# Hybrid decoder block on one core: the gate projections of two branches with three of eight pairs of k-tiles by Strassen's scheme

## The chip, the core and the metric

The kernel runs on one core of one Trainium2 chip, as a single launch. The metric is the device time of one execution in microseconds; lower is better. Before the change three runs gave 1595.34 us in the median (1595.19 to 1596.83).

## What is computed

One layer of a hybrid decoder block on x, 256 tokens of 2048 channels, with 256 memory tokens. All arrays are f32. Cut to what matters here:

```
h = rms_norm(x, g_mix_pre)
a_val, a_gate, sb, sc, sx, q, gates = split(h @ w_in)        # gates: three times 2048 columns

a = causal_depthwise_conv(a_val * sigmoid(a_gate), conv_a_w) + conv_a_b     # 31 taps
a = silu(layer_norm(a))
y_a = a @ w_a_out                                            # branch 0
y_b = (sb * causal_depthwise_conv(sc * sx, conv_b_w)) @ w_b_out   # branch 1, 3 taps
y_x = attention(q, memory) @ w_x_out                         # branch 2

g = sigmoid(gates)
merged = g[0] * y_a + g[1] * y_b + g[2] * y_x
x = x + rms_norm(merged @ w_o, g_mix_post)
x = x + rms_norm(relu(rms_norm(x) @ w_up)**2 @ w_down, g_mlp_post)
```

The three gate projections are [256, 2048] @ [2048, 2048] each, the three output products of the branches [256, 1024] @ [1024, 2048].

## The kernel before, in words

**Three products for one.** Every f32 operand of a matmul is split in an upper and a lower part that TensorE takes as fp32r: the upper one is a cast on ScalarE, the lower one the difference on VectorE. For weights `fetch_next` (L93) does this: SP loads a unit (two k-tiles of 128 rows by 512 columns) into a tile `raw`, ScalarE casts it to `wh` (L100), VectorE subtracts to `wl` (L101). For activations `split` (L221 to L223) does it. A product of a k-tile is then three matmuls: upper by upper, upper by lower, lower by upper.

**What sets the order.** The units are planned in the order in which they are used (`plan` L83, and the plan section behind L228). `in_unit` (L134) asks for a unit and fetches LOOK = 4 units ahead of it, in an order raised by PRIO; the tile framework then fixes each engine's instruction list when the kernel is built, and an engine runs its own list strictly in order. `raw` has RAW = 4 buffers, `wh` and `wl` five each. Between units, `between` (L119) issues one of the callables in `steps` and up to three taps of the long convolution (`tap` L449, the multiply-add L455), which are VectorE work on 128 x 256. `drain` (L130) issues all that is left in `steps`.

**The stages.** Queries, the conformer's inputs, keys, values and attention come first. Then branch 2 (L531) runs, then the short convolution (loop behind L531): per half i it projects `sc`, `sx` and `sb` into four banks each (`channels_first`), VectorE computes the three taps (L552 among them), adds the two halves of each `sb` bank (`halves`, L216 to L219), multiplies and splits into `uT[i]`. Then branch 1 (L607) and branch 0 (L627), the output projection and the MLP.

**A branch** (L522). `gates(b, n)` multiplies the 256 tokens by 512 gate columns over 16 k-tiles into two banks (`tokens_first`) and ScalarE takes the sigmoid (L507). `out_of(b, n)` multiplies the branch's activations by 512 columns over 8 k-tiles into two banks, and VectorE multiplies by the gate (L517 or L519) and adds (L520). The order is lagged: the gates of n + 1 stand ahead of the output product of n, so that in branch 0 the order is gates 0, gates 1, out 0, gates 2, out 1, and so on.

**LayerNorm of branch 0.** Behind branch 1 the remaining taps are issued, and then eight steps (L610) are appended: sum over channels (L573), mean by a matmul against ones and its subtraction (L579, L580), squares, variance, scale, sigmoid and gain (L600, L601), and the split into `aT[0]` and `aT[1]` (L223). They are issued between the units of the first gate blocks of branch 0, and `drain` issues the rest ahead of out 0.

```
    def branch(b, act, behind=lambda n: None):
        s = gates(b, 0)
        for n in range(4):
            s, last = gates(b, n + 1) if n < 3 else None, s
            if n == 0:
                drain()
            out_of(b, n, act, last)
            behind(n)
```

Of the kernel before, what the change touches and what calls it, by code (L numbers as in the profile page):

```python
# [15 lines left out]
P = 128  # L16
D = 2048
# [22 lines left out]
TAPS = 3  # L40
LOOK = 4
PRIO = 400
RAW = 4
# [3 lines left out]
def tile_hybrid_block(ctx, tc, x, head, xT, mem, memT, vecs, w_in, w_a_out, w_b_out, w_kv, w_x_out, w_o,  # L47
# [5 lines left out]
    big = ctx.enter_context(tc.tile_pool(name="big", bufs=14))  # L53
# [29 lines left out]
    def plan(w, row0, col0, nk=KD, sizes=None, gain=None):  # L83
        """[nk*128, 512] of w as units of some k-tiles each."""
# [53 lines left out]
    def mm_channels(acc, k, nk, wh, wl, a, ts=None):  # L138
        """Adds k-tile k to four banks, [128 columns of w, 256 tokens] in two halves each."""
# [75 lines left out]

    def halves(b, dst):  # L216
# [602 lines left out]
```

## Time and profile before

| what | value |
|---|---|
| median of three runs | 1595.34 us |
| the profiled execution, its span | 1595.4 us |
| TensorE busy | 1578.8 us, 7950 instructions |
| VectorE busy | 1096.3 us, 1621 instructions |
| ScalarE busy | 781.4 us, 1100 instructions |
| granted TensorE clock, mean | 0.998 |

The span is the time from the first to the last instruction of the profiled execution; no other time is given for that execution. PE is TensorE, DVE VectorE, ACT ScalarE, POOL GpSimd, SP SyncE, which issues the loads. In a timeline each row is a start, a length, the engine, the line of the kernel, the operation, output<-input tiles, their shapes and how many equal instructions the row joins; in brackets stands how long the engine had been idle before it, and what released it. A row that joins n instructions has the length from the first one's start to the last one's end.

### The profile page before, as it was taken

To read this page: it belongs to the slowest core of one execution; us is meant where nothing else is said; L and a number is where in the kernel's file an instruction comes from. 1 tells how busy PE (TensorE), PEld (TensorE's weight loads), DVE (VectorE), ACT (ScalarE), POOL (GpSimd) and SP (SyncE) were. 2 spreads that over 40 slices of the span, in tenths; PEclk is the share of its full clock that TensorE was granted. 3 is DMA by queue.
4 is the path that set the end of the run, shared out by engine and by line. 5 is a ranking of instruction groups with operands and counts; after the bars stand their busy time and mean duration, and the time that the engine had idled before them with its cause. 6 is when DMAs were issued, how large, how long until landed. Compare 5 with 4: busy or idle time off the path is not lost.

```text
span 1595.4 us, 21000 instructions
## 1 busy us (share of the span) xinstructions
PE 1578.8 (99%) x7950; PEld 1338.8 (84%) x7950; DVE 1096.3 (69%) x1621; ACT 781.4 (49%) x1100; POOL 7.6 (0%) x19
## 2 busy tenths in 40 slices
PE   8999999999999999999999999999999999999997
PEld 6888888888888888888888888888888888888886
DVE  6988787777898775775656775457755676567755
ACT  7654455443444444454445654455534554355542
POOL 0000000000000000000000000000000000000000
PEclk9999999999999999999999999999999999999999
DMA  8765655566666666666755665666666666666563
GB/s 274 218 212 185 192 165 172 174 196 189 189 188 187 189 194 197 185 187 191 263 191 168 204 190 190 194 190 185 188 194 197 185 185 192 192 191 188 188 193 111
DMA packets 158694, 305.64 MB, mean 192 GB/s; under 512 B 9473, under 2 KB 13825, under 8 KB 158081
## 3 DMA queue, kind: packets, MB, share of 16 engines
q1 hardware_dynamic: 158592, 304.30, 62.2%
q8 instruction: 62, 1.02, 0.3%
q14 instruction: 40, 0.32, 0.1%
HBM read 302.17 MB, written 2.10 MB: 191 GB/s over the span
## 4 chain that ended last, share of the span: by engine, by line
PE 98%; DVE 1%; DMA 0%; issue 0%; SPq 0%; ACT 0%; POOL 0%; POOLq 0%; DVEq 0%; ACTq 0%
PE bank L76 97%; DMA raw<-in_w_in 0%; DVE t L660 0%; PE bank L622 0%; DVE t L733 0%; DVE wl L106 0%; PE bank L668 0%; DVE t L223 0%; PE bank L420 0%; POOL y L320 0%; DVE t L647 0%; DVE wl L101 0%; ACT wh L100 0%; POOLq L815 0%; SPq L96 0%
## 5 line engine op out<-in xcount | busy, mean ns | idle before, releaser
L76 PE MATMUL bank<-wh,t 128*128 128x512 f32 (+1 forms) x2592 | 794.9, 387 | 0.0
L101 DVE TENSOR_TENSOR wl<-raw,wh 128x1024 fp32r<-128x1024 f32 (+1 forms) x433 | 528.1, 1221 | 366.4 <-ACT wh L100 364.5
L100 ACT CAST wh<-raw 128x1024 fp32r<-128x1024 f32 (+1 forms) x433 | 454.6, 1051 | 575.6 <-PE bank L76 513.7
L76 PE MATMUL bank<-t,wh 128*128 128x512 f32 (+1 forms) x1936 | 681.6, 398 | 4.7 <-ACT wh L100 4.7
L76 PEld LDWEIGHTS bank<-wh,t 128*128 128x128 f32 x2592 | 484.5, 188 | 97.9
L76 PE MATMUL bank<-t,wl 128*128 128x256 f32 (+1 forms) x1936 | 538.9, 281 | 1.6 <-ACT t L291 1.0
L76 PE MATMUL bank<-wl,t 128*128 128x512 f32 (+1 forms) x1296 | 500.9, 387 | 0.0
L76 PEld LDWEIGHTS bank<-t,wh 128*128 128x128 f32 x1936 | 364.1, 189 | 90.3 <-ACT wh L100 4.7
L76 PEld LDWEIGHTS bank<-t,wl 128*128 128x128 f32 x1936 | 367.4, 190 | 5.6 <-DVE wl L101 1.6
L76 PEld LDWEIGHTS bank<-wl,t 128*128 128x128 f32 x1296 | 243.4, 188 | 49.0
L106 DVE SCALAR_TENSOR_TENSOR wl<-raw,vec,wh 128x512 fp32r<-128x512 f32 x256 | 180.9, 748 | 88.8 <-ACT wh L105 86.7
L105 ACT ACTIVATE wh<-raw,vec 128x512 fp32r<-128x512 f32 x256 | 171.6, 717 | 138.5 <-PE bank L76 102.1
L455 DVE SCALAR_TENSOR_TENSOR t<-a_pad,vec,t 128x256 f32<-128x256 f32 x240 | 103.4, 478 | 0.0
L218 ACT COPY s<-bank 128x256 f32<-128x256 f32 x128 | 46.0, 366 | 15.8 <-PE bank L76 15.5
L219 DVE TENSOR_TENSOR s<-bank,s 128x256 f32<-128x256 f32 x128 | 52.3, 417 | 0.0
L222 ACT CAST t<-s 128x256 fp32r<-128x256 f32 x96 | 37.6, 400 | 23.3 <-DVE s L750 15.3
L223 DVE TENSOR_TENSOR t<-s,t 128x256 fp32r<-128x256 f32 x96 | 39.5, 419 | 6.4 <-ACT t L222 5.7
L748 DVE SCALAR_TENSOR_TENSOR s<-s,rm_bc 128x256 f32<-128x256 f32 x64 | 27.2, 426 | 2.2
L750 DVE TENSOR_TENSOR s<-s 128x256 f32<-128x256 f32 x64 | 27.1, 424 | 1.8
L507 ACT ACTIVATE s<-bank,y 128x512 f32<-128x512 f32 x24 | 16.4, 685 | 10.6 <-PE bank L76 10.6
L725 DVE TENSOR_TENSOR t<-bank,t 128x512 f32<-128x512 f32 (+1 forms) x25 | 15.7, 663 | 6.3 <-PE bank L76 6.3
L291 ACT ACTIVATE t<-t,vec 128x256 fp32r<-128x256 f32 x31 | 13.6, 498 | 4.2 <-DMA t<-in_memT 2.6
(105 smaller groups left out, 303.3 us busy)
## 6 DMA issues: line engine op xcount, KB each, us to landing
raw<-in_w_in SPq DMA_DIRECT2D x191, 512.0 KB, 3.8
raw<-in_w_up SPq DMA_DIRECT2D x128, 512.0 KB, 3.7
raw<-in_w_down SPq DMA_DIRECT2D x128, 512.0 KB, 3.7
raw<-in_w_kv SPq DMA_DIRECT2D x32, 512.0 KB, 3.8
raw<-in_w_o SPq DMA_DIRECT2D x32, 512.0 KB, 3.7
raw<-in_w_x_out SPq DMA_DIRECT2D x16, 512.0 KB, 3.9
raw<-in_w_b_out SPq DMA_DIRECT2D x16, 512.0 KB, 4.8
raw<-in_w_a_out SPq DMA_DIRECT2D x16, 512.0 KB, 4.0
```

What stands on the lines that cost most here:

```text
L76: nc.tensor.matmul(o, a, b, start=start, stop=stop)
L100: nc.scalar.copy(h, raw)
L101: pace[0] = nc.vector.tensor_tensor(l, raw, h.bitcast(F32), ALU.subtract).ins
L105: nc.scalar.mul(h[:, j, :], raw[:, j, :], g)
L106: pace[0] = nc.vector.scalar_tensor_tensor(l[:, j, :], raw[:, j, :], g, h[:, j, :].bitcast(F32), ALU.mult, ALU.subtract).ins
L218: nc.scalar.copy(t, b[:, T:])
L219: nc.vector.tensor_tensor(dst, b[:, :T], t, ALU.add)
L222: nc.scalar.copy(dst_h, src)
L223: nc.vector.tensor_tensor(dst_l, src, dst_h.bitcast(F32), ALU.subtract)
L455: nc.vector.scalar_tensor_tensor(conv[:, c, :], src, w, conv[:, c, :], ALU.mult, ALU.add)
L748: nc.vector.scalar_tensor_tensor(s, s, 0.0, r2_bc, ALU.max, ALU.mult)
L750: nc.vector.tensor_tensor(q, s, s, ALU.mult)
```

## The change

Branch order and block size change for all three branches; Strassen's scheme is used in branches 1 and 0.

- **Blocks of 1024 columns.** `gates(b, n)` and `out_of(b, n)` now take 1024 columns each, n = 0 and 1, with four accumulators (two token halves by two column halves), and they alternate: gates 0, out 0, gates 1, out 1. The lag is gone. The weights come in rows, one k-tile of 1024 columns for two k-tiles of 512, with the same size and number of loads. `RAW` is 5 in place of 4. The pool `big` has 13 buffers in place of 14: the gate s is a tile of `big` now, and a late constant `gq` uses the space of `a_pad`.
- **Three triples of k-tiles.** In a gate block of branches 1 and 0, k-tiles j and j + 8 for j = 0, 1, 2 are multiplied as 2 x 2 blocks with seven products in place of eight (the form of Strassen's scheme with common sums). With a the tokens (two halves t) and W the weights (two column halves q), the seven products are a(j, t0) W(j, q1) in `P1`; a(j+8, t0) W(j+8, q1) added to `C11`; form 3 by W(j+8, q0) added to `C12`; and form 0, 2, 1 and a(j+8, t1) by the four weight sums in `Q5`, `P7`, `P6` and added to `C21`. So a block has eight accumulators, all eight PSUM banks.
- **Weight sums.** `fetch_row` makes the four sums of 512 columns of a triple on VectorE (L125, L126, L129, L130), in two tiles that are then cast and split as any unit (L136, L137). Of the row "first" only one column half is used and split.
- **Forms of the tokens.** `x_forms`, once, ahead of branch 1: two additions that join upper and lower part of six k-tiles (L615), four sums and differences (L617 to L620), and a split (L329, L330) into `fh` and `fl`. It is appended to `steps` and drained before the first gate block.
- **Gathering.** `gather` (L306 to L320) adds the eight accumulators to the four results: two copies on ScalarE and eight additions or differences of 512 columns on VectorE; behind each of the four results stands its sigmoid on ScalarE.

```
+SUMMED = 3
+ORDER = (("row", 3), ("row", 11), ("first", 0), ("row", 4), ("second", 0), ("row", 5), ("sums_a", 0), ("row", 6),
+         ("sums_b", 0), ("first", 1), ("row", 7), ("second", 1), ("row", 12), ("sums_a", 1), ("row", 13), ("sums_b", 1),
+         ("first", 2), ("row", 14), ("second", 2), ("row", 15), ("sums_a", 2), ("sums_b", 2))
+TQ = ((0, 1), (0, 0), (1, 1), (1, 0))
-RAW = 4
+RAW = 5
...
-    big = ctx.enter_context(tc.tile_pool(name="big", bufs=14))
+    big = ctx.enter_context(tc.tile_pool(name="big", bufs=13))
...
+    def fetch_row(w, r0, c0, what):
...
+        if what[:4] == "sums":
+            a, b = held["first"], held["second"]
+            if what == "sums_a":
+                nc.vector.tensor_tensor(raw[:, 0], a[:, 0], a[:, 1], ALU.add)
+                nc.vector.tensor_tensor(raw[:, 1], a[:, 0], b[:, 0], ALU.add)
+                held["sums"] = raw
+            else:
+                nc.vector.tensor_tensor(raw[:, 0], held["sums"][:, 0], b[:, 0], ALU.add)
+                nc.vector.tensor_tensor(raw[:, 1], raw[:, 0], b[:, 1], ALU.add)
+        else:
+            nc.sync.dma_start(raw, w[r0:r0 + P, c0:c0 + 2 * NC5].rearrange("p (c n) -> p c n", c=2))
+            held[what] = raw
+            if what == "first":
+                part = slice(1, 2)
+        nc.scalar.copy(h[:, part], raw[:, part])
+        pace[0] = nc.vector.tensor_tensor(l[:, part], raw[:, part], h[:, part].bitcast(F32), ALU.subtract).ins
+        ready.append([(h[:, q], l[:, q]) for q in range(2)])
...
+    def block(rows, act, half, forms=None):
...
+        for n, (what, k, u) in enumerate(rows):
+            if what == "row":
+                todo += [(u, n, f"C{t + 1}{2 - q}", tile_of(k, t), q) for t, q in TQ]
+            elif what == "first":
+                todo.append((u, n, "P1", tile_of(k, 0), 1))
+            elif what == "second":
+                todo += [(u, n, "C11", tile_of(k + half, 0), 1), (u, n, "C12", form(k, 3), 0)]
+            elif what == "sums_a":
+                todo += [(u, n, "Q5", form(k, 0), 0), (u, n, "P7", form(k, 2), 1)]
+            else:
+                todo += [(u, n, "P6", form(k, 1), 0), (u, n, "C21", tile_of(k + half, 1), 1)]
...
+    def gather(acc, dst, put):
+        p1, u3 = (sm.tile([P, NC5], F32, tag="u512", name=name("u"), bufs=4) for _ in range(2))
+        nc.scalar.copy(dst(1, 0), acc["C22"])
+        nc.scalar.copy(p1, acc["P1"])
+        nc.vector.tensor_tensor(dst(0, 1), acc["C11"], p1, ALU.add)
+        put(0, 1)
+        nc.vector.tensor_tensor(p1, acc["P6"], p1, ALU.add)
+        nc.vector.tensor_tensor(u3, acc["P7"], p1, ALU.add)
+        nc.vector.tensor_tensor(dst(1, 1), acc["C21"], u3, ALU.add)
+        put(1, 1)
+        nc.vector.tensor_tensor(p1, acc["Q5"], p1, ALU.subtract)
+        nc.vector.tensor_tensor(dst(0, 0), acc["C12"], p1, ALU.add)
+        put(0, 0)
+        nc.vector.tensor_tensor(u3, acc["Q5"], u3, ALU.subtract)
+        nc.vector.tensor_tensor(dst(1, 0), dst(1, 0), u3, ALU.add)
+        put(1, 0)
...
+            g_gate[b, n] = plan_rows(w_in, C_G + b * D + n * 2 * NC5, ORDER if b < 2 else rows_of(16), 8)
+            g_y[b, n] = plan_rows(w, n * 2 * NC5, rows_of(8), 4)
...
+    def x_forms():
+        both, f = t8([P, 2, SUMMED, T]), t8([P, SUMMED, 4, P])
+        for i in range(2):
+            hl = xt[2 * i]
+            nc.vector.tensor_tensor(both[:, i], hl[:, :SUMMED, 0, :].bitcast(F32), hl[:, :SUMMED, 1, :].bitcast(F32), ALU.add)
+        a11, a21, a12, a22 = (both[:, i, :, t * P:(t + 1) * P] for i in range(2) for t in range(2))
+        nc.vector.tensor_tensor(f[:, :, 0, :], a21, a22, ALU.subtract)
+        nc.vector.tensor_tensor(f[:, :, 1, :], f[:, :, 0, :], a11, ALU.subtract)
+        nc.vector.tensor_tensor(f[:, :, 2, :], a11, a21, ALU.subtract)
+        nc.vector.tensor_tensor(f[:, :, 3, :], a12, f[:, :, 1, :], ALU.add)
+        fh, fl = t8([P, SUMMED, 4, P], F32R), t8([P, SUMMED, 4, P], F32R)
+        split(f, fh, fl)
+        xf.extend([fh, fl])
...
+        for n in range(2):
+            s = gates(b, n)
             if n == 0:
                 drain()
-            out_of(b, n, act, last)
-            behind(n)
+            out_of(b, n, act, s)
+            behind(2 * n)
+            behind(2 * n + 1)
...
+    steps.append(x_forms)
+    drain()
     branch(1, pair(uT))
```

**Excerpt one: VectorE's list where the short convolution ends and branch 1 begins.** Before: `bank_818` to `bank_821` are the four accumulators of the last `sb` projection, L219 adds their halves, L561 multiplies, L223 makes the lower part of `uT`, L101 that of a weight unit, L455 is a tap.

```order
L219 TENSOR_TENSOR s_847_4807<-bank_818_4614,s_848_4808 128x256
L561 TENSOR_TENSOR s_847_4807<-s_847_4807,t8_817_4597 128x256
L101 TENSOR_TENSOR wl_862_4858<-raw_860_4855,wh_861_4857 128x1024
L223 TENSOR_TENSOR t8_846_4806<-s_847_4807,t8_846_4806 128x256
L219 TENSOR_TENSOR s_849_4814<-bank_819_4615,s_850_4815 128x256
L219 TENSOR_TENSOR s_851_4821<-bank_820_4616,s_852_4822 128x256
L561 TENSOR_TENSOR s_849_4814<-s_849_4814,t8_817_4597 128x256
L561 TENSOR_TENSOR s_851_4821<-s_851_4821,t8_817_4597 128x256
L101 TENSOR_TENSOR wl_865_4879<-raw_863_4876,wh_864_4878 128x1024
```

The change, from the two sums of a weight row (L125, L126) on: L330 with `t8_844` is the lower part of `uT`, `t8_853` and `t8_854` are `both` and `f` of x_forms, `t8_855` and `t8_856` are `fh` and `fl`, L559 is a tap.

```order
L326 TENSOR_TENSOR s_849_4819<-bank_818_4614,s_850_4820 128x256
L326 TENSOR_TENSOR s_851_4826<-bank_819_4615,s_852_4827 128x256
L692 TENSOR_TENSOR s_849_4819<-s_849_4819,t8_815_4595 128x256
L692 TENSOR_TENSOR s_851_4826<-s_851_4826,t8_815_4595 128x256
L615 TENSOR_TENSOR t8_853_4833<-t8_2_77 128x768
...
L619 TENSOR_TENSOR t8_854_4834<-t8_853_4833 128x3x128
L617 TENSOR_TENSOR t8_854_4834<-t8_853_4833 128x3x128
...
L618 TENSOR_TENSOR t8_854_4834<-t8_854_4834,t8_853_4833 128x3x128
...
L620 TENSOR_TENSOR t8_854_4834<-t8_853_4833,t8_854_4834 128x3x128
...
L330 TENSOR_TENSOR t8_856_4842<-t8_854_4834,t8_855_4841 128x1536
```

The instructions of x_forms stand behind the last `sb` banks, and the lower part of the forms ends this piece; from the first of the four `sb` banks to it there are 28 instructions.

**Excerpt two: TensorE's list in the first gate block of branch 1.** `t8_2` and `t8_22` are k-tiles 0 to 3 and 8 to 11 of the tokens, `bank_861` to `bank_892` accumulators. Before, where the block begins:

```order
L76 MATMUL bank_821_4617<-t8_30_155,wh_832_4689 128x512
L76 MATMUL bank_855_4835<-wh_835_4714,t8_2_77 128x512
L76 MATMUL bank_855_4835<-wl_836_4715,t8_2_77 128x512
L76 MATMUL bank_855_4835<-wh_835_4714,t8_2_77 128x512
L76 MATMUL bank_856_4836<-wh_835_4714,t8_2_77 128x512
```

The change, 63 matmuls behind the block's first one:

```order
L83 MATMUL bank_866_4872<-wh_876_4919,t8_22_132 128x512
L83 MATMUL bank_866_4872<-wl_877_4920,t8_22_132 128x512
L83 MATMUL bank_866_4872<-wh_876_4919,t8_22_132 128x512
L83 MATMUL bank_865_4865<-wh_859_4847,t8_855_4841 128x512
L83 MATMUL bank_865_4865<-wl_860_4848,t8_855_4841 128x512
L83 MATMUL bank_884_4958<-wh_869_4890,t8_855_4841 128x512
L83 MATMUL bank_884_4958<-wl_870_4891,t8_855_4841 128x512
L83 MATMUL bank_865_4865<-wh_859_4847,t8_856_4842 128x512
```

The block took only the tokens' own tiles before; now its 22nd product reads the upper part of the forms (`t8_855`), and four matmuls later one reads the lower part (`t8_856`), the last result in excerpt one.

**Excerpt three: VectorE's list where the LayerNorm of branch 0 ends.** Before: L600 is the gain, L601 the last pass over all channels, L223 makes the lower part of `aT[0]` and `aT[1]`, L519 and L520 are the gated sum of out_of(0, 0).

```order
L600 TENSOR_SCALAR t8_37_190<-t8_37_190,vec_70 128x256 x4
L601 TENSOR_TENSOR t8_37_190<-t8_37_190,t8_1072_6026 128x2048
L101 TENSOR_TENSOR wl_1078_6065<-raw_1076_6062,wh_1077_6064 128x1024
L101 TENSOR_TENSOR wl_1082_6086<-raw_1080_6083,wh_1081_6085 128x1024
L223 TENSOR_TENSOR t8_1079_6080<-t8_37_190,t8_1079_6080 128x4x256
L101 TENSOR_TENSOR wl_1085_6104<-raw_1083_6101,wh_1084_6103 128x1024
L223 TENSOR_TENSOR t8_1086_6119<-t8_37_190,t8_1086_6119 128x4x256
```

The change; L434 is the copy of the scale over all partitions, L724 its pass, L731 and L732 are L600 and L601, L310 to L313 additions of `gather`, and L330 with `t8_1149` is the lower part of `aT[0]`.

```order
L434 COPY s_1126_6116<-bank_1127_6117 128x256
L724 TENSOR_TENSOR t8_37_190<-t8_37_190,s_1126_6116 128x2048
L137 TENSOR_TENSOR wl_1148_6217<-raw_1146_6215,wh_1147_6216 128x1024
L137 TENSOR_TENSOR wl_1152_6238<-raw_1150_6236,wh_1151_6237 128x1024
L137 TENSOR_TENSOR wl_1155_6250<-raw_1153_6248,wh_1154_6249 128x1024
L731 TENSOR_SCALAR t8_37_190<-t8_37_190,vec_70 128x256
L137 TENSOR_TENSOR wl_1161_6281<-raw_1159_6279,wh_1160_6280 128x1024
L731 TENSOR_SCALAR t8_37_190<-t8_37_190,vec_70 128x256 x7
L732 TENSOR_TENSOR t8_37_190<-t8_37_190,t8_1142_6176 128x2048
L310 TENSOR_TENSOR t8_1067_5881<-bank_1071_5888,u_1156_6260 128x512
L312 TENSOR_TENSOR u_1156_6260<-bank_1107_6031,u_1156_6260 128x512
L330 TENSOR_TENSOR t8_1149_6230<-t8_37_190,t8_1149_6230 128x4x256
```

Before, two gate blocks of 512 columns stood ahead of the first product with `aT`; now one block of 1024 columns does, and two additions of its gathering have come in front of the lower part of `aT[0]`.

## Rows read from the trace of the kernel before

**Rows 1.** The page: busy time by engine, and shares of the chain that ended last.
```profile
PE 1578.8 (99%) x7950; PEld 1338.8 (84%) x7950; DVE 1096.3 (69%) x1621; ACT 781.4 (49%) x1100; POOL 7.6 (0%) x19
...
PE 98%; DVE 1%; DMA 0%; issue 0%; SPq 0%; ACT 0%; POOL 0%; POOLq 0%; DVEq 0%; ACTq 0%
```

**Rows 2.** TensorE's timeline in a gate block of branch 0, first and last row.
```profile
743.06 0.62 PE L76 MATMUL bank<-wh,t 128*128 128x512 f32 x2
...
773.67 0.61 PE L76 MATMUL bank<-wh,t 128*128 128x512 f32 x2
```

**Rows 3.** VectorE's timeline: one row of each kind of instruction.
```profile
501.49 0.61 DVE L552 TENSOR_SCALAR t<-t,vec 128x256 f32<-128x256 f32 x2
...
521.18 0.75 DVE L219 TENSOR_TENSOR s<-bank,s 128x256 f32<-128x256 f32 x2
...
537.20 1.27 DVE L455 SCALAR_TENSOR_TENSOR t<-a_pad,vec,t 128x256 f32<-128x256 f32 x3
...
576.75 3.86 DVE L573 TENSOR_REDUCE s<-t 128x256 f32<-128x2048 f32 x1
580.53 3.48 DVE L101 TENSOR_TENSOR wl<-raw,wh 128x1024 fp32r<-128x1024 f32 x3
...
645.96 1.28 DVE L519 TENSOR_TENSOR s<-bank,s 128x512 f32<-128x512 f32 x2
...
684.34 2.29 DVE L601 TENSOR_TENSOR t<-t,t 128x2048 f32<-128x2048 f32 x1
686.55 2.35 DVE L101 TENSOR_TENSOR wl<-raw,wh 128x1024 fp32r<-128x1024 f32 x2
```

**Rows 4.** Timelines of VectorE and TensorE where branch 1 begins.
```profile
491.53 1.22 DVE L101 TENSOR_TENSOR wl<-raw,wh 128x1024 fp32r<-128x1024 f32 x1 [1.60 <-ACT wh L100]
...
518.91 0.42 DVE L219 TENSOR_TENSOR s<-bank,s 128x256 f32<-128x256 f32 x1
...
515.69 0.39 PE L76 MATMUL bank<-wh,t 128*128 128x512 f32 x1
```

**Rows 5.** Windows: length; busy PE, PEld, DVE, ACT, POOL; PEclk; DMA share; GB/s.
```profile
658.00:691.00 33.00, 33.00 (x151) 27.41 (x150) 29.37 (x30) 20.78 (x26) 0.69 (x1) 1.00 0.57 178
```

**Rows 6.** Timelines of VectorE and ScalarE around the LayerNorm of branch 0.
```profile
657.76 0.42 DVE L579 TENSOR_SCALAR s<-bank 128x256 f32<-128x256 f32 x1 [0.84 <-PE bank L76]
...
690.70 0.69 ACT L507 ACTIVATE s<-bank,y 128x512 f32<-128x512 f32 x1 [0.81 <-PE bank L76]
```

**Rows 7.** ScalarE's timeline: a cast of a unit, a pass over 2048 columns.
```profile
651.89 1.05 ACT L100 CAST wh<-raw 128x1024 fp32r<-128x1024 f32 x1 [1.67 <-PE bank L76]
...
661.48 1.91 ACT L584 ACTIVATE t<-t 128x2048 f32<-128x2048 f32 x1
```

**Rows 8.** TensorE's timeline at start and end, and windows behind its end.
```profile
12.78 0.58 PE L76 MATMUL bank<-t,wl 128*128 128x256 f32 x1 [0.64 <-DVE wl L101]
...
15.72 0.63 PE L76 MATMUL bank<-t,wh 128*128 128x512 f32 x1
16.36 0.56 PE L76 MATMUL bank<-t,wh 128*128 128x512 f32 x1
16.88 0.40 PE L76 MATMUL bank<-t,wh 128*128 128x512 f32 x1
17.23 0.40 PE L76 MATMUL bank<-t,wh 128*128 128x512 f32 x1
...
1586.51 0.28 PE L76 MATMUL bank<-wh,t 128*128 128x256 f32 x1
...
1589.00:1590.00 1.00, 0.00 (x0) 0.00 (x0) 0.68 (x2) 0.00 (x0) 0.29 (x1) 1.00 0.23 90
1590.00:1591.00 1.00, 0.00 (x0) 0.00 (x0) 1.00 (x2) 0.00 (x0) 0.00 (x0) 0.63 0.74 281
1591.00:1592.00 1.00, 0.00 (x0) 0.00 (x0) 1.00 (x2) 0.00 (x0) 0.00 (x0) 0.50 0.71 272
```

**Rows 9.** The page: DMA issues, KB each, median us from issue to landing.
```profile
raw<-in_w_in SPq DMA_DIRECT2D x191, 512.0 KB, 3.8
```

More of the change, by code (lines that the diff above doesn't have):

```diff
@@ L91, in plan, with plan_rows, rows_of, row_tiles @@
         return got
+    def plan_rows(w, col0, order, half):
+        got = []
+        for what, k in order:
+            units.append((w, (k + (half if what == "second" else 0)) * P, col0, (what,), None))
+            got.append((what, k, len(units) - 1))
+        return got
+    def rows_of(nk):
+        return tuple(("row", k) for k in range(nk))
+    held = {}
+    def row_tiles():
+        return (wp.tile([P, 2, NC5], F32, tag="raw", name=name("raw"), bufs=RAW),
+                wp.tile([P, 2, NC5], F32R, tag="wh", name=name("wh"), bufs=5),
+                wp.tile([P, 2, NC5], F32R, tag="wl", name=name("wl"), bufs=5))
+    def fetch_row(w, r0, c0, what):
+        raw, h, l = row_tiles()
+        part = slice(0, 2)
+        if what[:4] == "sums":
[15 more added lines that the diff above has]
+        ready.append([(h[:, q], l[:, q]) for q in range(2)])
     def fetch_next():
         w, r0, c0, s, gain = units[len(ready)]
+        if isinstance(s, tuple):
+            return fetch_row(w, r0, c0, *s)
         raw = wp.tile([P, s, NC5], F32, tag="raw", name=name("raw"), bufs=RAW)
@@ L214, in tokens_first, with tile_of, form @@
         return acc
+    def block(rows, act, half, forms=None):
+        todo = []
+        def tile_of(k, t):
+            return act(k)[:, 0, t * P:(t + 1) * P], act(k)[:, 1, t * P:(t + 1) * P]
+        def form(j, i):
+            h, l = forms
+            return h[:, j, i, :], l[:, j, i, :]
+        for n, (what, k, u) in enumerate(rows):
[9 more added lines that the diff above has]
+                todo += [(u, n, "P6", form(k, 1), 0), (u, n, "C21", tile_of(k + half, 1), 1)]
+        todo[:8] = sorted(todo[:8], key=lambda x: x[2])
+        last = {x[2]: i for i, x in enumerate(todo)}
+        acc = {}
+        for i, (u, n, c, (ah, al), q) in enumerate(todo):
+            wh, wl = in_unit(u)[q]
+            first = c not in acc
+            if first:
+                acc[c] = bank()
+            mm(acc[c], ah, wh, first, False)
+            mm(acc[c], ah, wl, False, False)
+            mm(acc[c], al, wh, False, i == last[c])
+            if i % 8 == 7:
+                between()
+        return acc
+    def gather(acc, dst, put):
[14 more added lines that the diff above has]
+        put(1, 0)
     def halves(b, dst):
@@ L501, in tile_hybrid_block @@
     m = [None, None]
[L503 to L507 removed]
+    xf = []
+    def x_forms():
[11 more added lines that the diff above has]
+        xf.extend([fh, fl])
@@ new lines, in gates, with put @@
+    def gates(b, n):
+        s = t8([P, 2, 2, NC5])
+        def put(t, q, src=None):
+            nc.scalar.activation(s[:, t, q, :], s[:, t, q, :] if src is None else src, AF.Sigmoid,
+                                 scale=r_of["x"][:, t:t + 1])
+        acc = block(g_gate[b, n], xg, 8, xf)
+        with soon():
+            if "P1" in acc:
+                gather(acc, lambda t, q: s[:, t, q, :], put)
+            else:
+                for t, q in TQ:
+                    put(t, q, acc[f"C{t + 1}{2 - q}"])
@@ L508, in gates @@
         return s
     def out_of(b, n, act, s):
-        y = tokens_first(g_y[b, n], act, nk=8)
-        if b == 2 and n % 2 == 0:
-            m[n // 2] = t8([P, 2, 2, NC5])
-        mn = m[n // 2][:, n % 2]
-        for t in range(2):
+        acc = block(g_y[b, n], act, 4)
+        if b == 2:
+            m[n] = t8([P, 2, 2, NC5])
+        for t, q in TQ:
+            y, mn, sn = acc[f"C{t + 1}{2 - q}"], m[n][:, q, t, :], s[:, t, q, :]
             if b == 2:
-                nc.vector.tensor_tensor(mn[:, t, :], y[t], s[:, t, :], ALU.mult)
+                nc.vector.tensor_tensor(mn, y, sn, ALU.mult)
@@ L518, in out_of @@
             else:
-                nc.vector.tensor_tensor(s[:, t, :], y[t], s[:, t, :], ALU.mult)
-                nc.vector.tensor_tensor(mn[:, t, :], mn[:, t, :], s[:, t, :], ALU.add)
+                nc.vector.tensor_tensor(sn, y, sn, ALU.mult)
+                nc.vector.tensor_tensor(mn, mn, sn, ALU.add)
     def branch(b, act, behind=lambda n: None):
-        s = gates(b, 0)
-        for n in range(4):
-            s, last = gates(b, n + 1) if n < 3 else None, s
+        for n in range(2):
+            s = gates(b, n)
```

12 lines of the change are left out of this document (1 added, 11 removed).

## The prediction

> **What bounds the kernel now.** I read the page's busy times and its chain first. TensorE is busy 1578.8 of 1595.4 us and the chain that ended last is 98% PE [rows 1]: a matmul taken away anywhere in the middle is worth its pitch, and a wait put into TensorE's list costs its full length. The pitch is in TensorE's timeline of a gate block: 135 matmuls of 512 columns start between 743.06 and 773.67, 0.2267 us each [rows 2]. VectorE is busy 69% over the span, but that is an average: in the 33 us that hold the LayerNorm of branch 0 it is busy 29.37 us [rows 5], and around the end of the short convolution it runs without a gap and late. Its last idle time ends at 491.53; TensorE starts the first gate block of branch 1 at 515.69, yet VectorE only then reaches the first bank of the projection before it, at 518.91, 3.2 us late [rows 4]. Today nobody waits for that lag, as the weight parts are cut several units ahead. So the question is not the sum of VectorE's work but whether TensorE's list now needs something from the end of a long piece of it.
>
> **What the change takes away.** A gate block had 16 k-tiles x 4 products; it has 10 x 4 + 3 x 7 = 61 products of three matmuls. That is 9 matmuls less in each of four blocks: 36 x 0.2267 = **8.2 us gained**, all on the path.
>
> **What it adds to VectorE.** Per block: 12 sums of 512 columns and 8 additions of the gathering, 20 x 0.60 = 12.0 us; 22 splits for 16, three of them half as wide (19 x 1.13 + 3 x 0.60 against 16 x 1.13), 5.2 us. Once: the seven instructions of x_forms. The prices are starts between neighbours [rows 3]: 0.60 for 512 columns, 1.13 for 1024, 2.2 for 2048, 0.34 for 256, 0.40 for a tap, 0.26 for a tensor_scalar, 3.78 for the reduce; estimates between these, 0.87 for 768, 0.47 for 384 and 1.67 for 1536. In all some 75 us on an engine with 499 us idle, so it would fit if it were spread. Three places decide.
>
> **Place A, the forms of x (excerpts one and two).** TensorE's list of the first block has 21 products, 63 matmuls or 14.3 us, before the first that takes a form. VectorE's list up to the sb banks is the same as before, plus four sums (2.4) and less half a split (0.5): so it reaches the first of these banks 3.2 + 1.9 = 5.1 us after the block starts. From there to the lower part of the forms stand 28 instructions: 4 splits 4.5, 2 sums 1.2, 12 of 256 columns 4.0, x_forms' 2 x 0.87, 4 x 0.47 and 1.67, three taps 1.2: 16.2 us. Before the last of them VectorE waits for ScalarE's cast of 1536 columns: between 1.05 for 1024 and 1.91 for 2048 [rows 7], I take 1.4, of which a tap hides 0.4, so about 1.1 with its hand-over. One sum needs a weight row whose load is issued only when a split four rows ahead is done; at 3.8 us to landing [rows 9] that is 0.4 later than VectorE gets there. The lower part is ready at 5.1 + 16.2 + 1.1 + 0.4 = 22.8, the upper one at 21.1. TensorE waits from 14.3 to 21.1, does four matmuls (0.9) and waits 0.8 more: **7.6 us lost**. If the lag were gone by then, 2.5; if the short dependent additions each cost a little more, 10.
>
> **Place B, the LayerNorm (excerpt three).** Its eight steps ran behind two gate blocks before; out_of(0, 0), which needs their result, now follows the first one. In the trace of before the first block starts at about 645.8, when the bank read at 645.96 [rows 3] is full. The mean is read 12.0 us later, at 657.76, and the product that needs the result comes about 44.5 us after that start, when the second gate block ends: the sigmoid that waited for its bank starts at 690.70 [rows 6]. Now it comes after 61 products, 41.5 us, and about 1.0 for the statistics' matmuls: at 42.5. VectorE reaches the mean at 12.5 at best, behind 48 matmuls and a full list. From there to the lower part of the first half of aT stand 43 instructions: 16 splits 18.1 and a half one 0.6, six sums 3.6, the reduce 3.8, three passes over 2048 columns 6.6, eight tensor_scalars 2.1, five small ones at up to 0.42 (as [rows 6]) 1.5, two additions of the gathering 1.2, and the lower part itself 1.1: 38.6 us. The last pass ends at 12.5 + 38.6 - 2.3 = 48.8, ScalarE's cast of 1.05 [rows 7] at about 49.9, the lower part at 51.1. TensorE waits 7.4 for the first, does two or three matmuls and waits 0.6 more: **8.0 us lost**. An earlier mean, right behind its matmul at 11.4, leaves 6.9; lists that stop for casts on the way make it 10.
>
> **Place C, the banks.** A block fills all eight. The output product behind it puts its first three accumulators in banks that one copy or the first addition sets free, and the fourth waits for the second addition (P6). 18 matmuls, 4.1 us, stand ahead of it, and that addition can start 0.7 us before the gate block ends. I cost it at nothing; without this cover it is the rival below.
>
> **What costs nothing.** The other three blocks: per block and its output product VectorE has 23.3 of splits, 7.2 of sums, 4.8 of gathering, 9.0 for the output's splits, 4.8 for the gated sum, 49 us against 63 us of TensorE (279 matmuls). Branch 1 has taps on top, but they stand behind splits there. The loads keep count and size (one row of 1024 columns for two tiles of 512), and SP waits for a free raw buffer as before: five now, of which a triple holds up to four. ScalarE adds six casts per block; it is not the later of the two at either place. Branch 2 keeps its products and its order of steps. For small waits I add nothing; half a microsecond here and there is in the range.
>
> **The clock.** Behind the last matmul, at 1586.51, the granted clock is still 1.00 (2.4 GHz) from 1589 to 1590, 0.63 in the next microsecond and then 0.50, 1.2 GHz [rows 8]. Waits of 7 us are longer than that. What a restart costs, no stretch in the middle of the run shows; the nearest is the start, where a pair of matmuls takes 0.64 us until 16.36 and 0.35 from 16.88 on [rows 8]. From the last gap, at 12.78, that is 3.6 us at the slow pace, 1.6 us lost; from the first matmuls, with the gaps taken out, some 10 us and 4.5 lost. I take 1.6 for each of the two waits, **3.2 us**, with 0 and 9 as ends. The Trainium skill, "TensorE: Matmul & The Clock Gate", section "HAM oscillation — how this bites in real kernels", says that a TensorE which waits long for operands falls to its half rate and starts every next burst slowly; by that rule each wait costs more than its length, and a version with few but long waits can lose what it saved. The end rows agree with the fall; no row of before shows the restart inside a kernel.
>
> **Sum.** -8.2 + 7.6 + 8.0 + 3.2 = +10.6. The profiled execution spans 1595.4 us, and the median of the three runs is 1595.34, so nothing lies around the span and the sum is made on it: **1606.0 us**. A difference under 0.2% (3.2 us) can't be told from none.
>
> **Rivals.**
> 1. *VectorE keeps up* (other side, faster). If the forms are ready when TensorE gets to them and the LayerNorm ends within its block, the 8.2 us stay: 1587.2. It decides at 14.3 us for the forms against my 21.1 and at 42.5 for aT against my 49.9. For it: VectorE's total is far from full. Against it: the lag of 3.2 us is in the trace, and the sums of 16.2 and 38.6 us hold no idle time. Half of it, one place hidden with its restart, gives about 1596.5. Chance 0.10 for all of it, 0.12 for half.
> 2. *The waits come without the clock falling*: 1602.8. For it: at A the first wait of 6.8 us is only about twice the time after which the clock fell at the end. Chance 0.18.
> 3. *The clock comes back late*, as from the kernel's first matmuls: 4.5 us twice, 1611.8. Chance 0.13.
> 4. *The gathering holds the banks*: if the fourth accumulator waited for all five additions (3.0 us) in each block, 12 us more, 1618. Against it: the order of the first accumulators. Chance 0.05.
> My forecast has 0.42.
>
> **Range and chances.** The forecast, rivals 2 and 3 and the ends of A and B (2.5 to 10, 6.9 to 10) reach from 1596 to 1617; what lies outside is rival 1 and most of rival 4. Faster by over 0.2% is rival 1, 0.10; half of it, near 1596.5, falls within 0.2%, 0.12; slower is the rest, 0.78.
>
> **What would show it.** TensorE's waits list should name two new long waits: for the upper part of the forms (ScalarE's cast, L329) of about 7 us some 14 us into the first gate block of branch 1, and for aT's cast of 7 us at the end of the first gate block of branch 0. TensorE should have 36 matmuls fewer; VectorE busy should be near 1170 us; VectorE's timeline should be without gaps ahead of both waits, and the granted clock below 1.00 behind them. No wait over 3 us on TensorE in the middle would make the forecast wrong; so would waits at the change from gates to output product.

## The result, and the profile after

The changed kernel takes **1613.49 us** (median of four runs, 1612.08 to 1615.86) against 1595.37 for the kernel before: ratio 1.0114, interval 1.0100 to 1.0128. It is 18.1 us slower. 1606.0 was forecast, with a range of 1596 to 1617.

The page of the profiled execution (time 1612.08, span 1610.3; in all runs listed with both, the time is 1.7 to 1.9 us above the span), busy times and chain:

```profile
PE 1574.9 (98%) x7914; PEld 1332.6 (83%) x7914; DVE 1167.9 (73%) x1732; ACT 805.4 (50%) x1133; POOL 8.5 (1%) x19
...
PE 90%; DVE 5%; DMA 2%; issue 2%; ACT 1%; POOL 0%; SPq 0%; POOLq 0%; DVEq 0%; ACTq 0%
```

Against [rows 1], TensorE has its 36 matmuls less and VectorE 71.6 us more, and the chain has left TensorE for a tenth of its length. TensorE's list of waits (what it waited for, sum, times, longest) names where; the kernel before has no wait on these lines:

```profile
PE bank L83 <- ACT t L329: 16.0, 2, 8.3
...
PE bank L83 <- DVE s L432: 1.3, 1, 1.3
PE bank L83 <- DVE wl L137: 1.1, 1, 1.1
PE bank L83 <- ACT u L309: 1.0, 1, 1.0
```

L329 is the cast in `split`: once of the forms, once of aT. TensorE's timeline at both places (last matmul before, first ones behind, and where the pitch of 0.2267 us is back):

```profile
513.52 0.39 PE L83 MATMUL bank<-wh,t 128*128 128x512 f32 x1
...
527.70 0.39 PE L83 MATMUL bank<-wh,t 128*128 128x512 f32 x1
535.77 0.79 PE L83 MATMUL bank<-wh,t 128*128 128x512 f32 x1 [7.68 <-ACT t L329]
...
539.97 0.62 PE L83 MATMUL bank<-wh,t 128*128 128x512 f32 x2
...
696.85 0.39 PE L83 MATMUL bank<-wh,t 128*128 128x512 f32 x1
705.54 0.79 PE L83 MATMUL bank<-wh,t 128*128 128x512 f32 x1 [8.30 <-ACT t L329]
...
710.15 0.62 PE L83 MATMUL bank<-wh,t 128*128 128x512 f32 x2
```

Behind each wait 11 matmuls take 4.20 and 4.61 us; at the pitch they take 2.49, so the restart costs 1.7 and 2.1 us more. The windows of the first place (length; busy PE, PEld, DVE, ACT, POOL; granted clock; DMA share; GB/s) show why:

```profile
531.00:532.00 1.00, 0.00 (x0) 0.00 (x0) 1.00 (x3) 0.00 (x0) 0.00 (x0) 1.00 0.00 0
532.00:533.00 1.00, 0.00 (x0) 0.00 (x0) 1.00 (x3) 0.00 (x0) 0.00 (x0) 0.62 0.00 0
533.00:534.00 1.00, 0.00 (x0) 0.00 (x0) 1.00 (x3) 0.00 (x0) 0.00 (x0) 0.50 0.00 0
...
538.00:539.00 1.00, 1.00 (x3) 0.73 (x3) 0.00 (x0) 0.56 (x1) 0.00 (x0) 0.50 0.00 0
539.00:540.00 1.00, 1.00 (x6) 0.81 (x5) 0.91 (x2) 0.55 (x2) 0.00 (x0) 0.97 0.00 0
```

TensorE stops at 528.1; its granted clock is still 1.00 from 531 to 532, 0.62 in the next microsecond, and then 0.50 (1.2 GHz) until 539. VectorE is busy through most of the gap: TensorE waits for work in progress, not for a transfer.

To account for the loss I take one stretch in both traces: from the first matmul of branch 1's first gate block (515.69 before [rows 4], 513.52 after) to the first transposes of the MLP:

```profile
866.81 0.66 PE L668 MATMUL bank<-ident,t 128*128 128x128 f32 x4 [0.51 <-DVE t L660]
```

```profile
881.48 0.66 PE L801 MATMUL bank<-ident,t 128*128 128x128 f32 x4 [0.51 <-DVE t L793]
```

That is 351.1 us before and 368.0 after, +16.8. The matmuls give -8.2, the two long waits 16.0, the three short ones 3.3, the half clock 3.8, together +14.9; the other 1.9 are pauses of a few tenths, behind the short waits above all, that no row names. I compare the stretch and not whole spans: the profiled execution before was some 1.8 us longer than the median run (its span of 1595.4 and the 1.8 us around it make 1597.2), and that of the change is the quickest of its four.

### The profile page after: what moved, and what is told of

The parts are those of the page before. It is cut to its first block, busy times and chain, and to the rows that moved or that the text cites. A ratio compares the mean times of both kernels' runs of the same rounds, so it can differ in the third digit from the quotient of the medians.

```text
span 1610.3 us, 21101 instructions
## 1 busy us (share of the span) xinstructions
PE 1574.9 (98%) x7914; PEld 1332.6 (83%) x7914; DVE 1167.9 (73%) x1732; ACT 805.4 (50%) x1133; POOL 8.5 (1%) x19
## 4 chain that ended last, share of the span: by engine, by line
PE 90%; DVE 5%; DMA 2%; issue 2%; ACT 1%; POOL 0%; SPq 0%; POOLq 0%; DVEq 0%; ACTq 0%
PE bank L83 89%; DVE wl L137 2%; DMA raw<-in_w_in 1%; DVE t L559 1%; ACT wh L136 0%; DMA t<-in_xT 0%; DMA raw<-in_w_b_out 0%; PE bank L755 0%; DVE t L793 0%; POOL y L424 0%; DVE raw L129 0%; DVE t L330 0%; DVE t L731 0%; ACT t L329 0%; DVE t L650 0%
## 5 line engine op out<-in xcount | busy, mean ns | idle before, releaser
L83 PEld LDWEIGHTS bank<-wh,t 128*128 128x128 f32 x2568 | 481.0, 188 | 115.1 <-ACT t L329 16.8
L150 DVE TENSOR_TENSOR wl<-raw,wh 128x1024 fp32r<-128x1024 f32 (+1 forms) x289 | 352.4, 1221 | 244.0 <-ACT wh L149 242.5
L149 ACT CAST wh<-raw 128x1024 fp32r<-128x1024 f32 (+1 forms) x289 | 303.5, 1051 | 376.7 <-PE bank L83 356.0
L136 ACT CAST wh<-raw 128x1024 fp32r<-128x1024 f32 (+1 forms) x168 | 169.0, 1023 | 172.5 <-PE bank L83 113.8
L137 DVE TENSOR_TENSOR wl<-raw,wh 128x1024 fp32r<-128x1024 f32 (+1 forms) x168 | 196.0, 1187 | 56.1 <-ACT wh L136 55.3
L559 DVE SCALAR_TENSOR_TENSOR t<-a_pad,vec,t 128x256 f32<-128x256 f32 x240 | 104.2, 482 | 0.0
L329 ACT CAST t<-s 128x256 fp32r<-128x256 f32 x96 | 37.6, 400 | 27.3 <-DVE s L883 15.3
L330 DVE TENSOR_TENSOR t<-s,t 128x256 fp32r<-128x256 f32 x96 | 39.6, 420 | 6.4 <-ACT t L329 5.7
```

Of the source, the lines that this page charges most:

```text
L83: nc.tensor.matmul(o, a, b, start=start, stop=stop)
L136: nc.scalar.copy(h[:, part], raw[:, part])
L137: pace[0] = nc.vector.tensor_tensor(l[:, part], raw[:, part], h[:, part].bitcast(F32), ALU.subtract).ins
L149: nc.scalar.copy(h, raw)
L150: pace[0] = nc.vector.tensor_tensor(l, raw, h.bitcast(F32), ALU.subtract).ins
L329: nc.scalar.copy(dst_h, src)
```

## The experiments

All kernels are the changed one with the edit named; ratios are to the kernel before on the same chip. Lines are numbered by each kernel's own text, so L329 is L330, L336 or L337 in some. Times at a glance:

| kernel | us | ratio, interval | longest new wait |
|---|---|---|---|
| the change | 1613.49 | 1.0114, 1.0100 to 1.0128 | 8.3 |
| early forms | 1604.33 | 1.0053, 1.0040 to 1.0065 | 8.3 |
| lag in branch 0 | 1612.06 | 1.0101, 1.0087 to 1.0115 | 7.9 |
| both of these | 1602.02 | 1.0042, 1.0029 to 1.0054 | 6.0 |
| no Strassen | 1595.28 | 0.9998, 0.9989 to 1.0007 | none |
| early, no sums in (0, 0) | 1599.44 | 1.0027, 1.0019 to 1.0036 | 8.3 |
| early, rows first in (0, 0) | 1604.59 | 1.0057, 1.0045 to 1.0070 | 9.4 |
| the same, no sums | 1600.62 | 1.0029, 1.0019 to 1.0038 | 9.5 |
| the same, LayerNorm first | 1599.86 | 1.0027, 1.0017 to 1.0037 | 2.4 |
| early, LayerNorm first | 1605.07 | 1.0061, 1.0048 to 1.0074 | 6.3 |
| late forms, rows first | 1605.09 | 1.0060, 1.0048 to 1.0073 | 9.7 |
| **early, (0, 0) plain** | **1591.99** | **0.9978, 0.9968 to 0.9987** | 0.7 |
| the same, four triples | 1596.46 | 1.0006, 0.9998 to 1.0015 | 3.1 |

**1. Early forms.** The theory is that of the prediction: two places at which VectorE is late.

```
     branch(2, pair(oT))
+    x_forms()
...
-    steps.append(x_forms)
```

> The forms of the tokens are made right behind branch 2, some 130 us before their first use; all else is the change. Theory: TensorE's wait of 7.7 us for the cast of the forms and the 1.7 us at the slow clock behind it vanish, the wait at the LayerNorm (8.3 us) stays: about 9 us less than the change's 1613.5, 1604. Rival 1: VectorE is late at that place anyway, and the wait only moves to a split or a weight sum of the same block: at most 3 us less, 1610 or more. Rival 2: only the length of the wait comes back and no clock: 1606.

1604.33. TensorE's timeline has 0.43 us left at place A:

```profile
529.07 0.47 PE L83 MATMUL bank<-wh,t 128*128 128x512 f32 x1 [0.43 <-DVE s L326]
```

Place A was worth its wait and its restart, 9.2 us; place B stands unchanged (8.3).

**2. Lag in branch 0.** Order gates 0, gates 1, out 0, out 1.

```
+        if b == 0:
+            for n in range(2):
+                g_y[b, n] = plan_rows(w, n * 2 * NC5, rows_of(8), 4)
...
+        s = [gates(b, n) for n in range(2)] if b == 0 else [gates(b, 0), None]
```

> In branch 0 both gate blocks stand ahead of both output products, so that the LayerNorm has 83 us of TensorE's work and not 41; all else is the change. Theory: the wait of 8.3 us for the cast of aT goes with its 2.1 us at the slow clock, and with it the small waits of the statistics: 10 to 13 us less than the change's 1613.5, 1601 to 1603; the wait for the forms stays at 7.7. Rival: VectorE is full in the Strassen blocks themselves, so that the passes of the LayerNorm push splits and sums late and TensorE waits for these in several pieces: 1606 or more.

1612.06: a miss, by some 10 us. The wait for aT is gone, but another stands where the first gate block ends:

```profile
PE bank L83 <- DVE t L310: 6.0, 1, 6.0
```

L310 is the first addition of the gathering. The second gate block needs a bank that this addition frees, and it stands in VectorE's list behind the LayerNorm. So the LayerNorm delays whoever needs VectorE behind it: once through aT, once through the banks.

**3. Both edits.**

> Both edits, early forms and the two gate blocks of branch 0 ahead of its output products. Theory: both long waits go, the 36 matmuls less (8.2 us) remain: 1588 to 1593, below the kernel before (1595.4). Rival: the layout costs something beside the two waits (a bank, a load, VectorE's load): between 1596 and 1602.

1602.02, on the upper end of the rival's range: the wait at L310 is again 6.0.

**4. No Strassen, same layout.**

```
-            g_gate[b, n] = plan_rows(w_in, C_G + b * D + n * 2 * NC5, ORDER if b < 2 else rows_of(16), 8)
+            g_gate[b, n] = plan_rows(w_in, C_G + b * D + n * 2 * NC5, rows_of(16), 8)
...
-    steps.append(x_forms)
```

> The change's blocks of 1024 columns, order, five raw buffers and pool, but no Strassen: all gate blocks have 16 plain rows, no weight sums, no forms, no gathering. Theory: the scheme's own VectorE work makes both waits. So none at the first gate block of branch 1, and 0 to 3 us at the LayerNorm, which still has one gate block of TensorE work only: 1595 to 1599. Rival: the new order of blocks alone makes the LayerNorm late, with a wait of 5 us or more there: 1602 to 1606.

1595.28, no difference from the kernel before, and no wait in the stretch, though out_of(0, 0) follows one gate block here too. Blocks of 1024 columns, the order without lag and five raw buffers cost nothing; the scheme makes both waits. Whether by its work on VectorE or by its eight open banks this run can't tell, as it takes away both.

**5. Early forms, no sums in (0, 0).** What holds the LayerNorm? VectorE's list alone, or also the banks: in the change the matmul of its variance waited for `L309`, the copy that frees P1's bank.

```
+        if what[:4] == "sums" and c0 == C_G:
+            raw = held["first"]
```

> Early forms as in the run before, and in the gate block (0, 0) alone the weight sums are left out: its six tiles of sums are casts and splits of the row already loaded, so the gates of the first 1024 columns of branch 0 are not the reference's. That takes 12 additions of 0.6 us, 7.2 us, from VectorE in the stretch of the LayerNorm and leaves banks, matmuls and splits as they are. Theory 1, VectorE is full there: the wait of 8.3 us for aT's cast shrinks to about 1, and the time to some 1595. Theory 2, the eight banks: the matmul of the variance still waits for the copy of P1 some 12 us before the block ends, and what is left behind it takes its 13 us anyhow; the wait stays at 5 or more: 1600 to 1602.

1599.44, as theory 2 had it, a little better. ScalarE's copy of P1 (L316 here), and in TensorE's timeline the matmul of the variance, which starts when the copy is done, and the one that needs aT:

```profile
674.30 0.57 ACT L316 COPY u<-bank 128x512 f32<-128x512 f32 x1
...
674.96 0.58 PE L83 MATMUL bank<-ones,s 128*128 128x1 f32 x4
...
692.84 0.80 PE L83 MATMUL bank<-wh,t 128*128 128x512 f32 x1 [8.31 <-ACT t L336]
```

7.2 us less on VectorE takes away the short waits and 4.9 us of the time, and nothing of the long one.

**6. Early forms, rows first in (0, 0).**

```
+ROWS_FIRST = tuple(x for x in ORDER if x[0] == "row") + tuple(x for x in ORDER if x[0] != "row")
...
+(ROWS_FIRST if (b, n) == (0, 0) else ORDER)
```

> Early forms, and in the gate block (0, 0) the ten plain rows stand ahead of the three triples, so that for 40 products only four of eight banks are taken and the variance finds a bank; VectorE's work is the same. Theory 2, banks: the LayerNorm is done inside the block, no long wait, 1591 to 1595. Theory 1, VectorE is full: its work for the block is 51 us (23 splits, 7 sums, 5 gathering, 16 LayerNorm) against 41.5 of TensorE; what is not late for aT is late for the splits and sums of the triples at the end: waits of 6 us or more in all, 1599 or more.

1604.59, against theory 2. The variance comes at once, 11 us earlier than with early forms alone (677.49), and aT comes no earlier:

```profile
666.32 0.61 PE L84 MATMUL bank<-ones,s 128*128 128x1 f32 x4 [0.40 <-DVE s L706]
...
697.62 0.79 PE L84 MATMUL bank<-wh,t 128*128 128x512 f32 x1 [9.39 <-ACT t L330]
```

**7. The same without the sums.**

> Early forms, plain rows first in the gate block (0, 0), and its weight sums left out, so its gates are not the reference's. Both suspected causes are out of the block at once: the variance finds a bank, and VectorE has 7.2 us less. Theory 3, that each of the two alone holds the LayerNorm back: the wait of 9.4 us with rows first shrinks by 7.2 to some 2, about 9 us less than that run: 1595 to 1597. If 6 us or more stay, neither the bank nor the amount of VectorE's work decides, but where the LayerNorm's passes stand in VectorE's list.

1600.62; the wait is 9.5. Less work brings 4.0 us against experiment 6, in short waits and pauses; the long wait goes neither with the bank free, nor with less work, nor with both. VectorE's timeline of this kernel shows what is left (L145 is the split of a weight unit, L740 and L741 the LayerNorm's last passes, L338 the lower part of aT):

```profile
668.88 1.23 DVE L145 TENSOR_TENSOR wl<-raw,wh 128x1024 fp32r<-128x1024 f32 x1 [1.34 <-ACT wh L144]
...
674.10 7.50 DVE L145 TENSOR_TENSOR wl<-raw,wh 128x1024 fp32r<-128x1024 f32 x7
681.51 0.41 DVE L740 TENSOR_SCALAR t<-t,vec 128x256 f32<-128x256 f32 x1
681.83 1.22 DVE L145 TENSOR_TENSOR wl<-raw,wh 128x1024 fp32r<-128x1024 f32 x1
...
688.10 1.23 DVE L145 TENSOR_TENSOR wl<-raw,wh 128x1024 fp32r<-128x1024 f32 x1 [1.05 <-ACT wh L144]
689.24 2.02 DVE L740 TENSOR_SCALAR t<-t,vec 128x256 f32<-128x256 f32 x6
691.30 2.29 DVE L741 TENSOR_TENSOR t<-t,t 128x2048 f32<-128x2048 f32 x1
...
694.84 1.22 DVE L338 TENSOR_TENSOR t<-t,t 128x1024 fp32r<-128x1024 f32 x1
```

VectorE even has gaps at 668; then it does seven splits in a row, and five more among the LayerNorm's passes, because units are issued ahead of steps (PRIO). Its last splits belong to the output product, which can't use them before aT, and the last of these waits for a cast that waits for its load:

```profile
687.02 1.04 ACT L144 CAST wh<-raw 128x1024 fp32r<-128x1024 f32 x1 [0.73 <-DMA raw<-in_w_a_out]
```

Plain rows hide that: four products use a unit, 2.7 us of TensorE for a split of 1.13. In a triple seven products use four units, 1.2 us each. There the units fetched ahead fill VectorE's list, and what has no priority comes last. This is read from the timeline; experiment 8 tests it.

**8. Rows first, LayerNorm first.** The eight steps are issued ahead of the units.

```
+    def first(step):
+        def go():
+            with soon():
+                step()
+        return go
+
+    steps += [first(s) for s in (lambda: channel_sum(conv), ln_mean, ln_square, ln_var, ln_scale, swish,
```

> Early forms, plain rows first in the gate block (0, 0), all sums kept, and the eight LayerNorm steps issued with a higher priority than the weight units: the lower part of aT then stands 25 instructions earlier in VectorE's list, ahead of the splits and sums of the triples and of the first units of the output product. VectorE's work is the same. If the amount of work decides (51 us in 41.5), what the LayerNorm gains the splits lose: waits of 6 us or more in other places, 1600 or more. If the place in the list decides, since the units split ahead are a reserve of some 10 us: no wait over 2 us, 1589 to 1593.

1599.86: the wait for aT is gone, so its place in the list made it; but six shorter waits of 0.5 to 2.4 us came in its place, 7.0 in all, so that the first expectation nearly holds as well. Five of them, 4.7 us, lie in the gate block (0, 0) and the product behind it, where VectorE is busy 27.6 of 30 us. The longest lies elsewhere: the priority has also drawn the LayerNorm's first sum over channels (L706) forward into branch 1, from 602.37 in experiment 6 to 583.23, and a gated sum (L651) whose bank TensorE needs stands behind it:

```profile
583.23 3.90 DVE L706 TENSOR_REDUCE s<-t 128x256 f32<-128x2048 f32 x1
...
595.34 0.50 PE L84 MATMUL bank<-wh,t 128*128 128x512 f32 x1 [2.36 <-DVE t L651]
```

So a third of the 7.0 us comes from where this edit puts the steps, and not from a full VectorE at the LayerNorm. The price of these waits is their length and the pauses behind them, some 3 us: the granted clock stays 1.00, also around the longest (windows as above).

```profile
594.00:598.00 4.00, 2.66 (x12) 2.18 (x13) 4.00 (x6) 0.96 (x1) 0.00 (x0) 1.00 0.53 167
...
680.00:710.00 30.00, 26.48 (x110) 19.91 (x109) 27.62 (x32) 18.30 (x21) 0.00 (x0) 1.00 0.73 234
```

**9. LayerNorm first, rows in the change's order.** The fourth corner: priority without a free bank.

> Early forms and the LayerNorm's steps issued ahead of the weight units, but the rows of the gate block (0, 0) in the change's order, so that all eight banks are taken from its 27th product on. If the place in VectorE's list alone decided, the long wait goes as it did with plain rows first: about 1600. If the banks hold the LayerNorm as soon as the list does not, the matmul of the variance still waits for P1's copy, some 12 us before the block ends, and its remaining chain (two passes of 2.2, eight small ones, cast, two hand-overs through GpSimd and TensorE) takes 12 to 14 us from there: a wait of 2 to 6 us stays for aT's cast, 1600 to 1604.

1605.07, 1 us above the second expectation. The bank holds it: the sum that the variance's matmul takes (L705) is done at 663.4, and the matmul waits for P1's copy 18 us later:

```profile
659.50 3.87 DVE L705 TENSOR_REDUCE s<-t 128x256 f32<-128x2048 f32 x1
...
681.73 0.61 PE L83 MATMUL bank<-ones,s 128*128 128x1 f32 x4 [2.23 <-ACT u L309]
...
698.68 0.79 PE L83 MATMUL bank<-wh,t 128*128 128x512 f32 x1 [6.26 <-ACT t L329]
```

So each of the two is enough to make aT late: 8.3 with both, 9.4 with the list alone, 6.3 with the bank alone, none with neither. The wait of branch 1 that experiment 8 brought is here too, with 2.0 us.

**10. Late forms, rows first in both first blocks.**

```
+(ROWS_FIRST if n == 0 else ORDER)
```

> Forms made late, as in the change, but the first gate block of both branches has its ten plain rows ahead of the triples. The first product with a form then comes 42 products, 28.6 us, into the block, and the forms were ready 22.3 us into it: theory, no wait for them, and about the time of the run with early forms and rows first in (0, 0) alone. Rival: the sums of three triples in a row, 6.4 us of VectorE for each 4.8 us of TensorE, make waits of 3 us or more at each of the two blocks' ends.

1605.09, the time of experiment 6, so A can be hidden by order as well as by an early start. In the block of branch 1 short waits of 0.3 and 1.1 us are left, less than the rival's 3, and two of 0.7 and 0.6 later in branch 1; at the LayerNorm it is experiment 6 again, 9.7.

**11. Early forms, (0, 0) plain.**

```
+ORDER if b == 1 or (b, n) == (0, 1) else rows_of(16)
```

> Early forms, and the gate block (0, 0) has 16 plain rows; the other three gate blocks keep the scheme. Nine matmuls (2.0 us) come back. Both theories: with four banks free and 16 splits in place of 22 and 12 sums the LayerNorm hides, no wait over 1 us: 1604.3 less about 13 plus 2.0, some 1593. If a wait of 5 us or more stays, the block in front of the first output product is too short for the LayerNorm whatever it computes.

**1591.99**, 3.3 us below the kernel before and 21.5 below the change: the scheme where VectorE has room, and none where the LayerNorm stands. Its waits in the stretch come to 0.7 us, and the stretch is 4.6 us shorter than before, of the 6.1 that 27 matmuls are worth.

**12. The same with four triples.**

```
-SUMMED = 3
+SUMMED = 4
```

> Early forms, a plain gate block (0, 0), and in the other three gate blocks four triples in place of three: three matmuls less per block, 9 x 0.2267 = 2.0 us, for four more sums (2.4 us) and a row's split less on VectorE per block. Theory, TensorE is the bound in these blocks: 2 us less than with three triples (1592.0), 1590. Rival, VectorE is full in branch 1, where taps stand between: waits of 1 us or more eat it, 1592 or more.

1596.46, on the rival's side, but not by its cause. In branch 1 a split of weight sums came 3.1 us late, and two splits and a cast some 0.5 each. The last tap had started at 592.7; what stands ahead of the late split is the LayerNorm's first sum over channels (L706), which runs in this block. The split's cast was done at 617.3. Two rows of VectorE's timeline, one of TensorE's, and a window behind the wait:

```profile
616.63 3.74 DVE L706 TENSOR_REDUCE s<-t 128x256 f32<-128x2048 f32 x1
...
620.90 1.21 DVE L138 TENSOR_TENSOR wl<-raw,wh 128x1024 fp32r<-128x1024 f32 x1
...
622.16 0.79 PE L84 MATMUL bank<-wl,t 128*128 128x512 f32 x1 [3.11 <-DVE wl L138]
...
626.00:627.00 1.00, 1.00 (x4) 0.81 (x3) 0.29 (x2) 0.84 (x1) 0.00 (x0) 0.50 1.02 401
```

The granted clock fell in this wait as well: the 14 matmuls from 622.16 to 628.38 take 6.2 us where the pitch makes 3.2. The wait and the 3.0 us behind it are more than the 4.5 us that this kernel is slower than experiment 11, where the same sum, at 601.23, made nobody wait. Four triples with this sum in another place were not run, so it stays open whether they pay.

## Why the prediction was right, and where its size was off

**Matmuls, -8.2:** right; 36 instructions are gone, at the pitch of [rows 2].

**Place A, 7.6:** right in place, cause and size, 7.68, with one piece of luck. VectorE reached the first `sb` bank 5.1 us into the block, as forecast, and the lower part of the forms was done 24.0 us into it (22.8 forecast); the load cost 0.7 and not 0.4, the cast 1.47 and not 1.4:

```profile
518.63 0.42 DVE L326 TENSOR_TENSOR s<-bank,s 128x256 f32<-128x256 f32 x1
...
526.72 0.69 DVE L126 TENSOR_TENSOR raw<-raw,raw 128x512 f32<-128x512 f32 x1 [0.72 <-DMA raw<-in_w_in]
...
535.75 1.76 DVE L330 TENSOR_TENSOR t<-t,t 128x1536 fp32r<-128x1536 f32 x1 [1.20 <-ACT t L329]
```

The sum had two waits, 6.8 us for the upper part and 0.8 for the lower. The first came out 0.9 longer; the second did not come, as the four matmuls between them ran at half clock (1.9 us in place of 0.9) and the lower part was done by then. Experiment 1 shows the place by itself.

**Place B, 8.0:** right in size, 8.30, but by two errors that cancel, and the sum behind it was too simple. From the mean to the end of the last pass VectorE needed 39.9 us, where the sum had 36.3 (38.6 less the lower part and its neighbours, 2.3):

```profile
664.49 0.42 DVE L710 TENSOR_SCALAR s<-bank 128x256 f32<-128x256 f32 x1
...
702.12 2.29 DVE L732 TENSOR_TENSOR t<-t,t 128x2048 f32<-128x2048 f32 x1
```

Counted from the block's first matmul, at 650.05, the last pass ended at 54.4 us and not 48.8, and TensorE came to aT at 47.2 and not at 42.5, as its block grew by its own short waits; so the difference of the two stayed. That the sums hold no idle time is the step that fell: VectorE stood idle for 2.6 of the 39.9 us, waiting for casts and for GpSimd. And the amount of work is not what makes aT late: 7.2 us less of it left the long wait as it was and was worth 4 to 5 us in short ones (experiments 5 and 7); the place of the passes behind the units, and the bank, make it late (experiments 8 and 9).

**Place C and the small waits, 0:** this is the term that was mis-sized. I looked for the banks behind the block, where 18 matmuls cover them, and not inside: with eight accumulators open the LayerNorm's own matmuls have no bank. The change's timeline has three waits of this stretch, 3.3 us, and 1.9 us of pauses come with them:

```profile
675.10 0.50 PE L83 MATMUL bank<-wl,t 128*128 128x512 f32 x1 [1.06 <-DVE wl L137]
686.13 0.61 PE L83 MATMUL bank<-ones,s 128*128 128x1 f32 x4 [0.98 <-ACT u L309]
690.85 0.68 PE L83 MATMUL bank<-s,ones 128*128 128x128 f32 x4 [1.26 <-DVE s L432]
```

Rival 4, the gathering that holds the banks of the next product, did not come in the change; a wait of its kind, for the first addition and not for all five, came in experiments 2 and 3, when another full block followed.

**The clock, 3.2:** 3.8 measured. The Trainium skill, "TensorE: Matmul & The Clock Gate", section "HAM oscillation — how this bites in real kernels", has long operand waits followed by a slow start; this trace agrees, with 1.7 and 2.1 us lost at 0.50; experiment 8 shows waits of up to 2.4 us without it, and experiment 12 one of 3.1 us with it.

**Base of the sum:** that nothing lies around the span was wrong. Time and span differ by 1.7 to 1.9 us in every run that lists both, and the profiled execution was some 1.8 us slower than the median run; the two errors cancel.

The rest of the miss of 7.5 us (18.1 measured, 10.6 forecast) is thus 5.2 of short waits and pauses, 1.0 at A, B and the clock, and 1.3 outside the stretch of the two profiled executions: that of the change starts the stretch 2.2 us earlier, but lies 1.4 below its median, and that of before lies 1.8 above its own. The time measured is nearest to rival 3's 1611.8, but not by its cause, as the clock cost 3.8 us and not 9; that it lies in the range is owed to the room that rival 3 and the far ends of A and B gave it.

## What to carry to other kernels

Fewer matmuls paid for with work on another engine are worth their pitch only where that engine's list has room in the same block; so apply such a scheme block by block, and leave out the one in which a long chain has to finish. Ask of each operand not only how much work stands before it, but what the scheduler puts ahead of it (units fetched early for a consumer that itself waits for this operand) and which bank it needs while all are open. What a wait costs beyond its length is not in proportion to it, and has to be read behind each: here waits of up to 2.4 us left the clock at 1.00 and cost pauses of a few tenths, one of 3.1 us cost another 3.0 at half clock, and those of 7.7 and 8.3 another 1.7 and 2.1. And look where a priority, or the framework, puts the long steps of a later chain: a sum of 3.7 us stands right ahead of the wait that took experiment 12's gain.

## What had not been expected of the hardware

The part ahead of the stretch differs by some 2 us between executions: the first gate block of branch 1 starts at 515.69 in the profiled run before and at 513.52 in that of the change, though 2672 matmuls stand ahead of it in both. The whole of the 2.17 us is there by the 500th matmul. At the start of the kernel the pace of a pair of matmuls goes from 0.64 to 0.35 us at about 13.5 us in the change, and at about 16.6 in the kernel before [rows 8]:

```profile
13.18 0.51 PE L83 MATMUL bank<-t,wh 128*128 128x512 f32 x1
...
13.64 0.40 PE L83 MATMUL bank<-t,wh 128*128 128x512 f32 x1
13.99 0.39 PE L83 MATMUL bank<-t,wh 128*128 128x512 f32 x1
```

Three microseconds longer at the slow pace are 1.4 us, an estimate from the two paces, and [rows 8] has a wait of 0.64 us at 12.78 that the change lacks; the two nearly make the difference. Why the clock rises earlier in one execution than in another was not tried.
